# A written-out transfer order: other groups of tiles, in another order

## The chip, the cores and the metric

One core of a Trainium2 chip runs the whole problem. The metric is the time of one launch on the device in microseconds (us), smaller is better. A core has five engines with a queue of instructions each: TensorE (PE in the profile) multiplies and transposes, VectorE (DVE) and ScalarE (ACT) and GpSimd (POOL) work on elements, and SyncE (SP) issues the transfers here. Sixteen DMA engines move the data between the chip's memory (DRAM) and the on-chip buffer. Each transfer of this kernel is spread over all sixteen.

## The reference

```
x:         16 x 512 x 1024  float32      weight: 1024 x 768  float32
add_value: 16 x 512 x 768   float32      scale = 0.1
out = (scale * matmul(x, weight) + add_value)   float32, 16 x 512 x 768
```

The rows of the sixteen batches form one matrix of 8192 rows. So the kernel reads 33.6 MB of x, 25.2 MB of add_value and 3.1 MB of weight, and writes 25.2 MB of out.

## The kernel before, in words

**Tiles.** The 8192 rows are cut into 64 tiles of 128 rows. Partition p holds rows 64p to 64p+63, and tile t is row 64p+t of each partition (lines 57 to 59). Tiles that follow each other therefore lie side by side in DRAM within each partition: one transfer of n tiles of x takes one contiguous run of n times 4 KB for each of the 128 partitions, and n times 3 KB for add_value and out. In the trace each such run is one packet.

**Rings.** x is loaded into `xs`, a ring of 24 slots (X_SLOTS, line 23); tile t uses slot t modulo 24. add_value is loaded into `ao`, another ring of 24 slots (A_SLOTS). VectorE writes the result over the add_value that it read, in the same slot, and the store of out leaves from there. So a slot of `xs` is free again when its tile has been cast, and a slot of `ao` only when the store of the tile 24 before has landed.

**The order of transfers** is written out by hand in `STREAM` (lines 12 to 21): ("x", s, n) loads tiles s to s+n-1 of x, "a" the same of add_value, "w" one of the eight slices of weight (through slots 16 to 23 of `ao`), "o" stores tiles of out, and "l" and "r" store the two column parts of the last tile. The loop at line 231 walks through it. It issues every transfer on SyncE (lines 93, 241, 247 and 255), and ahead of a transfer it emits as many computing steps as must have been emitted before: for an "x" over slots used earlier, until the old tiles have been cast (line 237); for an "o", until its last tile is finished (line 251). SyncE works in order: a transfer that waits for its slots holds up all transfers behind it. The order of instructions on the other engines is nearly independent of `STREAM`; what changes is when their data arrives.

**The steps.** The first three tiles (EARLY) are multiplied weight slice by weight slice as the weights arrive (function `head`), and their scaled product waits in slots 13 to 15 of `ao` until add_value comes (`added`, line 228). Every later tile is a `step` (line 204). Sixteen matmuls (`product`, line 161) multiply the tile with the weight, and in the middle of them the next tile is turned: GpSimd casts it to bf16 (line 129), TensorE transposes it in four pieces (line 139), ScalarE copies it out of PSUM (line 145). For the eighteen tiles in `PAIRS` VectorE turns the tile instead (lines 102 and 113). Then VectorE scales, adds and writes (`finish`, line 169). Products have three PSUM buffers, so TensorE can run up to about two tiles ahead of a `finish` that waits for add_value.

Of the kernel before, what the change touches and what calls it, by code (L numbers as in the profile page):

```python
# [11 lines left out]
STREAM = [  # L12
    ("x", 0, 1), ("x", 1, 1), ("x", 2, 1), ("w", 0, 1), ("w", 1, 1), ("w", 2, 1),
    ("w", 3, 1), ("w", 4, 1), ("w", 5, 1), ("x", 3, 1), ("w", 6, 1), ("w", 7, 1),
    ("a", 0, 3), ("x", 4, 3), ("a", 3, 7), ("x", 7, 3), ("x", 10, 6), ("a", 10, 6),
    ("x", 16, 8), ("a", 16, 8), ("x", 24, 7), ("o", 0, 8), ("o", 8, 8), ("a", 24, 5),
    ("x", 31, 7), ("a", 29, 4), ("x", 38, 5), ("a", 33, 5), ("o", 16, 8), ("x", 43, 5),
    ("a", 38, 7), ("x", 48, 8), ("o", 24, 8), ("a", 45, 3), ("a", 48, 6), ("o", 32, 8),
    ("x", 56, 8), ("a", 54, 6), ("o", 40, 8), ("o", 48, 4), ("a", 60, 4), ("o", 52, 6),
    ("o", 58, 4), ("o", 62, 1), ("l", 63, 1), ("r", 63, 1),  # L20
]

X_SLOTS = 24
# [267 lines left out]
```

## Time and profile before

| what | us |
|---|---|
| median of four runs (213.49, 213.86, 214.08, 215.13) | 213.97 |
| the profiled execution's own time | 213.49 |
| its span, first to last instruction | 211.7 |
| what lies around the span | 1.8 |
| TensorE busy in the span | 195.7 |
| mean rate of the transfers over the span | 412 GB/s |
| bytes moved by SyncE's queue | 87.03 MB |

How it is read: the profile is one execution. Busy times of engines overlap, so they are compared with the span and not added up. The queue row of the profile gives the share of the span in which the sixteen DMA engines had a packet of that queue in work. The windows view gives the same for stretches of the span, with the granted share of TensorE's clock in the third column from the right. The chain of waits follows back from the last instruction what released each step.

### The profile page before, as it was taken

To read this page: it belongs to the slowest core of one execution; us is meant where nothing else is said; L and a number is where in the kernel's file an instruction comes from. 1 tells how busy PE (TensorE), PEld (TensorE's weight loads), DVE (VectorE), ACT (ScalarE), POOL (GpSimd) and SP (SyncE) were. 2 spreads that over 40 slices of the span, in tenths; PEclk is the share of its full clock that TensorE was granted. 3 is DMA by queue.
4 is the path that set the end of the run, shared out by engine and by line. 5 is a ranking of instruction groups with operands and counts; after the bars stand their busy time and mean duration, and the time that the engine had idled before them with its cause. 6 is when DMAs were issued, how large, how long until landed. Compare 5 with 4: busy or idle time off the path is not lost.

```text
span 211.7 us, 3011 instructions
## 1 busy us (share of the span) xinstructions
PE 195.7 (92%) x1195; PEld 119.9 (57%) x1218; DVE 130.8 (62%) x223; ACT 49.3 (23%) x52; POOL 63.4 (30%) x69
## 2 busy tenths in 40 slices
PE   7777499999999999999999999999999997999991
PEld 2544356666565666566566665565656664655650
DVE  1447113359788699679786983699787981053241
ACT  3503112333203113013031121130230310313310
POOL 1310505290260260900804407105408102713000
PEclk9999669999999999999999999999999999999999
DMA  6999999999999999999999999999999999999984
GB/s 243 390 424 426 450 430 404 433 456 418 441 409 424 446 441 410 430 431 418 435 418 442 442 427 432 429 421 437 362 352 410 440 443 404 428 404 428 437 374 190
DMA packets 6637, 87.21 MB, mean 412 GB/s; under 512 B 736, under 2 KB 864, under 8 KB 2656
## 3 DMA queue, kind: packets, MB, share of 16 engines
q1 hardware_dynamic: 6624, 87.03, 97.9%
q8 instruction: 9, 0.15, 0.3%
q14 instruction: 4, 0.03, 0.0%
HBM read 61.87 MB, written 25.17 MB: 411 GB/s over the span
## 4 chain that ended last, share of the span: by engine, by line
DMA 54%; PE 40%; SPq 2%; DVE 1%; issue 1%; POOL 0%; POOLq 0%; DVEq 0%
DMA out_dram<-ao 37%; PE mm L161 35%; DMA ao<-in_add_value_dram 7%; DMA xs<-in_x_dram 6%; PE tp L139 5%; DMA ao<-in_weight_dram 3%; DVE ao L169 1%; SPq L241 1%; POOL xb L129 0%; SPq L93 0%; SPq L247 0%; SPq L255 0%; POOLq L129 0%; DVEq L169 0%
## 5 line engine op out<-in xcount | busy, mean ns | idle before, releaser
L161 PE MATMUL mm<-w_bf,xt 128*128 128x256 bf16 (+1 forms) x719 | 129.2, 329 | 3.7 <-DVE w_bf L97 1.3
L161 PEld LDWEIGHTS <-xt 128*128 128x128 bf16 x736 | 69.5, 99 | 53.2 <-ACT xt L145 10.8
L169 DVE SCALAR_TENSOR_TENSOR ao<-mm,ao 128x768 f32<-128x768 f32 (+2 forms) x62 | 58.3, 944 | 62.0 <-PE mm L161 30.8
L145 ACT COPY xt<-tp 128x1024 bf16<-128x1024 bf16 (+1 forms) x49 | 46.6, 961 | 152.0 <-PE tp L139 151.9
L113 DVE STREAM_TRANSPOSE vt<-vx 32x256 f32<-32x256 f32 x144 | 62.7, 435 | 2.9 <-POOL vx L102 0.7
L129 POOL CAST xb<-xs 128x1024 bf16<-128x1024 f32 x43 | 43.3, 1040 | 44.5 <-DMA xs<-in_x_dram 36.5
L161 PE MATMUL mm<-w_bf,vt 128*128 128x256 bf16 (+1 forms) x282 | 49.1, 325 | 0.3
L102 POOL CAST vx<-xs 128x1024 bf16<-128x1024 f32 x18 | 18.2, 1040 | 81.5 <-DVE vt L113 46.9
L161 PEld LDWEIGHTS <-vt 128*128 128x128 bf16 x288 | 28.2, 98 | 17.5
L139 PE MATMUL tp<-identity,xb 128*128 128x128 f32 x184 | 28.6, 279 | 6.0 <-POOL xb L129 5.1
L139 PEld LDWEIGHTS tp<-identity,xb 128*128 128x128 f32 x184 | 22.2, 145 | 12.6 <-POOL xb L129 5.8
L97 DVE CAST w_bf<-ao 128x768 bf16<-128x768 f32 x8 | 4.5, 562 | 4.7 <-DMA ao<-in_weight_dram 4.7
L87 PE MATMUL warm<-zeros 128*128 128x512 bf16 x10 | 4.4, 628 | 1.2 <-DVE zeros L75 1.2
L125 DVE CAST xb<-xs 128x512 bf16<-128x512 f32 x3 | 1.3, 426 | 5.1 <-DMA xs<-in_x_dram 5.1
L87 PEld LDWEIGHTS <-zeros 128*128 128x128 bf16 x10 | 1.3, 140 | 3.4 <-issue 2.2
L127 POOL CAST xb<-xs 128x512 bf16<-128x512 f32 x2 | 1.7, 866 | 5.0 <-DMA xs<-in_x_dram 5.0
L228 DVE TENSOR_TENSOR ao<-ao 128x768 f32<-128x768 f32 x3 | 2.7, 948 | 0.0
L197 DVE TENSOR_SCALAR ao<-mm 128x768 f32<-128x768 f32 x2 | 1.8, 952 | 1.1 <-PE mm L161 1.1
L127 ACT ACT_TABLE_LOAD x1 | 1.3, 1283 | 0.7 <-PEq L272 0.7
L127 ACT CAST xb<-xs 128x512 bf16<-128x512 f32 x1 | 0.6, 618 | 2.1 <-DMA xs<-in_x_dram 2.1
L194 ACT ACTIVATE ao<-mm 128x768 f32<-128x768 f32 x1 | 0.8, 817 | 0.0
L75 DVE MEMSET zeros<- 128x256 uint32 x1 | 0.3, 272 | 0.9 <-PEq L272 0.9
(6 smaller groups left out, 0.9 us busy)
## 6 DMA issues: line engine op xcount, KB each, us to landing
out_dram<-ao SPq DMA_DIRECT2D x6, 3072.0 KB, 25.6
xs<-in_x_dram SPq DMA_DIRECT2D x3, 4096.0 KB, 26.6
xs<-in_x_dram SPq DMA_DIRECT2D x2, 3584.0 KB, 33.3
ao<-in_add_value_dram SPq DMA_DIRECT2D x3, 2304.0 KB, 15.8
ao<-in_add_value_dram SPq DMA_DIRECT2D x2, 2688.0 KB, 16.0
xs<-in_x_dram SPq DMA_DIRECT2D x2, 2560.0 KB, 30.5
ao<-in_add_value_dram SPq DMA_DIRECT2D x2, 1920.0 KB, 19.1
ao<-in_weight_dram SPq DMA_DIRECT2D x8, 384.0 KB, 7.6
```

The lines of the kernel that those rows point to most:

```text
L87: nc.tensor.matmul(warm[:, 0:CUT], zeros[:, 0:P], zeros, start=True, stop=True)
L97: nc.vector.tensor_copy(w_bf[:, j + i, :], ao[:, s + i, :])
L102: nc.gpsimd.tensor_copy(vx[:, i, :], xs[:, (t0 + i) % X_SLOTS, :])
L113: nc.vector.transpose(vt[b:b + 32, :, 32 * a:32 * a + 32], pairs[32 * a:32 * a + 32, :, b:b + 32])
L127: other(xb[:, K // 2:K], src[:, K // 2:K])
L129: nc.gpsimd.tensor_copy(xb, src)
L139: nc.tensor.transpose(tp[:, c, :], pairs[:, c * P:(c + 1) * P], identity)
L145: nc.scalar.copy(dst[:, c:c + q, :, :], src[:, c:c + q, :, :])
L161: nc.tensor.matmul(mm_tiles[t, cols[0]][:, n0:n1], lhs(t, j), w_bf[:, j, n0:n1], start=(j == 0), stop=(j == KJ - 1))
L169: nc.vector.scalar_tensor_tensor(a, mm_tiles[t, part][:, n0:n1], float(scale), a, op0=mybir.AluOpType.mult, op1=mybir.AluOpType.add)
L228: nc.vector.tensor_add(ao[:, t, :], ao[:, EARLY_AT + t, :], ao[:, t, :])
L241: nc.sync.dma_start(xs[:, k:k + n, :], x_v[:, s:s + n, :])
```

## The change

Only `STREAM` is changed, from its thirteenth entry on; everything else, line numbers included, stays. The head (three tiles of x, weight, a fourth tile of x, the first three tiles of add_value) and the last three stores are the same. Between them the tiles are cut otherwise: loads and stores of x, add_value and out now hold four or eight tiles and begin at a tile number, and so at a ring slot, that is a multiple of four, except for one load of a single add_value tile (tile 3) and a store of two tiles at the end. The order among loads of x, loads of add_value and stores is another one as well. There are 47 transfers in place of 46.

```
-    ("a", 0, 3), ("x", 4, 3), ("a", 3, 7), ("x", 7, 3), ("x", 10, 6), ("a", 10, 6),
-    ("x", 16, 8), ("a", 16, 8), ("x", 24, 7), ("o", 0, 8), ("o", 8, 8), ("a", 24, 5),
-    ("x", 31, 7), ("a", 29, 4), ("x", 38, 5), ("a", 33, 5), ("o", 16, 8), ("x", 43, 5),
-    ("a", 38, 7), ("x", 48, 8), ("o", 24, 8), ("a", 45, 3), ("a", 48, 6), ("o", 32, 8),
-    ("x", 56, 8), ("a", 54, 6), ("o", 40, 8), ("o", 48, 4), ("a", 60, 4), ("o", 52, 6),
-    ("o", 58, 4), ("o", 62, 1), ("l", 63, 1), ("r", 63, 1),
+    ("a", 0, 3), ("x", 4, 4), ("a", 3, 1), ("a", 4, 4), ("x", 8, 4), ("x", 12, 4),
+    ("a", 8, 8), ("x", 16, 8), ("a", 16, 8), ("x", 24, 8), ("o", 0, 8), ("o", 8, 8),
+    ("a", 24, 4), ("x", 32, 4), ("a", 28, 8), ("a", 36, 4), ("x", 36, 8), ("o", 16, 8),
+    ("x", 44, 4), ("a", 40, 8), ("x", 48, 4), ("o", 24, 8), ("x", 52, 8), ("a", 48, 4),
+    ("o", 32, 8), ("a", 52, 4), ("a", 56, 8), ("x", 60, 4), ("o", 40, 8), ("o", 48, 8),
+    ("o", 56, 4), ("o", 60, 2), ("o", 62, 1), ("l", 63, 1), ("r", 63, 1),
```

## The prediction

> **What bounds the kernel now.** I read the page's totals and its queue row, then the rate in stretches, then the waits of SyncE, then TensorE's timeline, then single packets.
>
> ```profile
> span 211.7 us, 3011 instructions
> PE 195.7 (92%) x1195; PEld 119.9 (57%) x1218; DVE 130.8 (62%) x223; ACT 49.3 (23%) x52; POOL 63.4 (30%) x69
> ...
> q1 hardware_dynamic: 6624, 87.03, 97.9%
> ```
>
> Both the DMA engines (97.9%) and TensorE (92%) are nearly full, so I have to find which of them sets the end. The stretches (wall time, busy time of each engine, granted clock, DMA share, GB/s):
>
> ```profile
> 23.10:29.92 6.82, 5.87 (x20) 3.39 (x22) 0.00 (x0) 1.01 (x1) 2.64 (x3) 0.50 1.00 425
> ...
> 60.00:90.00 30.00, 29.79 (x189) 18.54 (x192) 24.57 (x45) 6.07 (x6) 11.79 (x12) 1.00 1.00 425
> 90.00:120.00 30.00, 29.79 (x189) 18.46 (x192) 24.47 (x45) 6.07 (x6) 9.97 (x11) 1.00 1.01 430
> ...
> 150.00:160.00 10.00, 9.95 (x64) 6.05 (x64) 7.84 (x16) 3.04 (x3) 0.74 (x2) 1.00 1.00 350
> 160.00:180.00 20.00, 18.44 (x117) 11.21 (x117) 13.18 (x23) 3.04 (x3) 5.83 (x7) 1.00 1.00 430
> ```
>
> The rate is 425 to 430 GB/s for most of the run and 350 in 150 to 160. That hole is worth (430-350)/430 x 10 = 1.9 us. What stands there:
>
> ```profile
> 122.71 0.38 SPq L255 DMA_DIRECT2D out_dram<-ao  x1
> 123.14 28.42 SPq L247 DMA_DIRECT2D ao<-in_add_value_dram  x2
> 151.66 0.37 SPq L255 DMA_DIRECT2D out_dram<-ao  x1
> ```
>
> SyncE issues a(45,3) at 123.14 and holds a(48,6) until 151.23, because tiles 48 to 53 take the slots of o(24,8), which lands only then. Behind that store just 2.8 us of work is queued, a(45,3). Most DMA engines run dry and start again together at 152.2.
>
> TensorE has only these pauses after 24 us:
>
> ```profile
> 23.83 1.11 PE L139 MATMUL tp<-identity,xb 128*128 128x128 f32 x4 [3.61 <-POOL xb L129]
> ...
> 179.94 0.66 PE L139 MATMUL tp<-identity,xb 128*128 128x128 f32 x4 [1.45 <-POOL xb L129]
> ...
> 185.74 1.46 PE L161 MATMUL mm<-w_bf,xt 128*128 128x512 bf16 x8 [0.78 <-DVE ao L169]
> ```
>
> The first waits for x(4,3); the two late ones (2.23 us) are x(56,8) and a(54,6) arriving late after the hole.
>
> **Prices from packets.** A packet of 4096 B usually takes 159 ns, 12288 B 460, 24576 B 912, 32768 B 1213: 27.2 GB/s an engine plus 8 ns. An odd size at an odd slot costs no more: most packets of a(10,6) (slot 10, 18432 B) take 686 to 694 ns against 686 by the formula. An engine has 8 packets of each transfer and a 9 ns semaphore write. Its share is 5,439,488 B, 200.0 us; 46 x 8 x 8 ns = 2.9 and 46 x 9 ns = 0.4 make 203.3.
>
> The engine that ends last is behind this running sum by 4.3 us at 30 us (1.7 us start, slow first packets, instruction fetches of about 1 us), 4.1 at 150.7, 6.3 at 161.2 (end of a(48,6)), 7.1 at 199.3 and 7.0 at its end, 210.34. Its packets of a(48,6) took 7.7 us where 5.5 are due, and a(54,6) and a(60,4) cost 0.9 more. So the last DMA engine sets the end, and 3.05 us of it is slow reads after 151. TensorE would allow an earlier end: its last store is issued at 207.41, and the engines that lag least are through with it at 208.95, 1.54 later.
>
> **What the skill says.** "DMA: Bandwidth & Descriptors", "Where 436 GB/s comes from", puts the ceiling of sixteen engines at 435 GB/s; 16 x 27.2 = 435 agrees, so larger transfers can gain only the 8 ns a packet. The same page, "Why a DMA increments its semaphore by 16 and not by 1", says that a transfer counts as landed when the last of its engines is done; the trace agrees: o(24,8) landed at 151.22, while the first engine had gone on at 148.63. "TensorE: Matmul & The Clock Gate", Part 1, says that TensorE runs at half clock after an idle window of some 3.4 us and needs a busy window to recover; the trace agrees, with 0.50 from 23.10 to 29.92 around a pause of 3.61 us.
>
> **The change, part by part.**
>
> *Packets.* 47 transfers for 46: one more time 73 ns. The sum becomes 203.41. Larger groups save nothing in number.
>
> *x(4,4) for x(4,3).* 16 KB for 12 KB a packet is +1.22 us until the first of these tiles can be cast, so TensorE restarts at 25.05 and not 23.83. If the half clock still ends at 29.92, it costs (29.92-25.05)/2 = 2.43 instead of 3.05. Net for TensorE: +0.6; +1.2 if the window shifts with the restart.
>
> *The front.* a(8,8) waits for `added` like a(10,6) did (22.2), but 15 us of loads are queued by then. x(8,4) lands by about 34.7 (sum 30.15 + 4.1 + 0.45 from last packet to semaphore), needed for tile 8 at 40. x(24,8) waits for one cast more, tile 7, about 28; the queue reaches to 61.
>
> *The waits in the middle.* For each load held by a store, I compare that store's landing (running sum + 4.55; the first engine is through at sum + 2.0) with the work queued behind it:
> - a(28,8) waits for o(8,8): sum 83.67, landing 88.2. a(24,4) and x(32,4) behind it keep the first engine busy until 94.2.
> - a(40,8) waits for o(16,8): 120.25, landing 124.8. x(44,4) keeps it busy until 127.1; the new packets need 1.0 after issue (151.23 to 152.19), so 125.8. Margin 1.3.
> - a(48,4) waits for o(24,8): 144.64, landing 149.2, and x(52,8) (9.7 us) is queued, to 156.3. This is where the old order ran dry; margin 6.
> - a(56,8) waits for o(32,8): 165.34, landing 169.9, first packets 170.9; a(52,4) ends on the first engine at 171.0. Margin 0.1, the tightest.
>
> So the hole at 151 is gone and a near one stands at 171.
>
> *TensorE's supply.* x(36,8) lands at 117.5; casts of 39 and 40 (2.1 us) go before that of 36 on GpSimd, so its transpose can start at 120.7, due about 121.0: margin 0.3. x(60,4) lands at 185.8 against 193.8. a(48,4) lands at 162.6, 2 us after tile 48's product, which the PSUM buffers cover. SyncE's extra issue (0.4) lies under queued work. The two late pauses go: 206.94-2.23+0.6 = 205.3 for TensorE's last matmul, last store issued 205.8, done 207.3.
>
> *The end.* Last DMA engine: 203.41+4.05+e = 207.46+e, where e is what slow reads are left. That is next late after TensorE's 207.3. The unknown is e: 0 if the common restart made the packets slow, 3.05 if they come anyway. I take 0.4, half of what a(54,6) and a(60,4) showed, because before 150 reads of every size were at full rate. So 207.9; +1.33 from last packet to span's end (211.68-210.34) = 209.2; +1.82 = 211.0 against 213.49 of the profiled execution. The median lies 0.48 above that execution, so I predict 211.4.
>
> **Rivals.**
> - *The stall moves to 171* (24%). A margin of 0.1 is less than the spread of the engines; they run dry there and a(56,8) reads as slowly as a(48,6) did. e = 3 again: 210.5+1.33+1.82+0.48 = 214.1, no change. For it: the same shape of wait. Against: only the first engines idle, and for tenths.
> - *TensorE becomes the bound* (8%). The longer pause keeps the clock at half one window more, 3.41 us, which costs 1.7: last matmul 207.0, store done 209.05, time 212.2+0.48 = 212.7. That still is slightly faster.
> - *Slow reads belong to the late tiles of add_value* (16%). All slow loads after 150 are of tiles 48 and up, while x(56,8) ran at full rate. At a(48,6)'s 2.23/6 = 0.37 us a tile, a(48,4), a(52,4) and a(56,8) would cost 16 x 0.37 = 5.9: 207.46+5.9+3.63 = 217.0, slower. It is slower than the 0.5% bound from 0.25 us a tile on (e = 4). Against it: a(54,6) and a(60,4) cost only 0.09 a tile.
> - *Alignment itself counts.* If slots or multiples of four changed packet times, a(10,6) would show it; it doesn't, so I give it nothing.
>
> **The numbers.** Forecast 52%, alone 210.5 to 212.6 (e from 0 to about 1.2, with or without the median's offset); the rivals as given. Range 210.3 to 214.8, into the first and last rival. A measurement here can tell about 0.5% (1.1 us) from no change. Faster 0.60 (forecast and TensorE's), no change 0.24, slower 0.16.
>
> **What would show it.** Right: no wait of the DMA engines near 150, rates of 425 or more between 150 and 180, no pause of TensorE after 26 us, last matmul near 205.3. Wrong: a rate under 400 after 150, above all in a(56,8); TensorE pausing at 120 for x(36,8); half clock beyond 31.

## The result, and the profile after

The changed kernel takes 213.45 us (median of 40 executions, 211.14 to 216.88) against 214.25 us of the kernel before (61 executions, 212.69 to 216.27). The ratio is 0.9939, 95% interval 0.9922 to 0.9957. Ratios here leave out executions more than 1.5% above their kernel's fastest (11 of these 40, 3 of the 61), while medians and the lowest and highest are of all, so a kernel with many long executions looks better by its ratio than by its median. By the medians alone it is 0.9963: the kernel is faster, by some 0.4 to 0.6%. Forecast was 211.4; of a gain of 2.6 us, 0.8 came. The profiled execution took 212.23 us, span 210.3.

The totals of the page, of the changed kernel:

```profile
span 210.3 us, 3009 instructions
PE 194.9 (93%) x1195; PEld 119.2 (57%) x1218; DVE 131.2 (62%) x223; ACT 49.3 (23%) x52; POOL 63.5 (30%) x69
...
q1 hardware_dynamic: 6768, 87.03, 98.2%
```

Both full resources are a little fuller. The stretches of the changed kernel (columns as before: wall, five engines, granted clock, DMA share, GB/s):

```profile
60.00:90.00 30.00, 29.79 (x189) 18.52 (x192) 24.57 (x46) 6.07 (x6) 11.77 (x13) 1.00 0.99 423
90.00:120.00 30.00, 29.79 (x190) 18.50 (x192) 22.91 (x42) 6.07 (x6) 8.49 (x9) 1.00 1.01 432
...
150.00:160.00 10.00, 9.95 (x66) 6.15 (x66) 7.84 (x15) 3.04 (x3) 0.74 (x1) 1.00 0.98 420
160.00:170.00 10.00, 9.95 (x66) 6.14 (x65) 6.90 (x13) 2.02 (x2) 6.31 (x7) 1.00 1.00 427
170.00:180.00 10.00, 9.95 (x65) 6.26 (x64) 6.67 (x11) 1.73 (x2) 1.72 (x2) 1.00 1.00 392
180.00:190.00 10.00, 9.89 (x65) 6.16 (x65) 3.14 (x4) 3.33 (x4) 2.80 (x4) 1.00 1.02 420
```

The hole of 150 to 160 (350 GB/s before) is filled: 420. A new one stands in 170 to 180, at 392. SyncE's issues there:

```profile
149.78 20.60 SPq L247 DMA_DIRECT2D ao<-in_add_value_dram  x2
170.47 0.76 SPq L241 DMA_DIRECT2D xs<-in_x_dram  x1
171.32 34.11 SPq L255 DMA_DIRECT2D out_dram<-ao  x7
```

a(52,4) goes out at 149.78, a(56,8) only at 170.05, when o(32,8) has landed. Its first packets start at 171.01. Four of the packets of a(56,8) took 2.8 to 3.0 us and two more 2.3 to 2.5, where 0.91 is due.

TensorE has one pause left after 19 us, the one for x(4,4):

```profile
24.82 1.12 PE L139 MATMUL tp<-identity,xb 128*128 128x128 f32 x4 [4.82 <-POOL xb L129]
```

From there to its last matmul it does not stop for longer than 0.25 us. The late pauses of 1.45 and 0.78 us are gone.

### The profile page after: what moved, and what is told of

It reads as the page before. It is cut to its first block, busy times and chain, and to the rows that moved or that the text cites. A ratio compares the mean times of both kernels' runs of the same rounds, so it can differ in the third digit from the quotient of the medians.

```text
span 210.3 us, 3009 instructions
## 1 busy us (share of the span) xinstructions
PE 194.9 (93%) x1195; PEld 119.2 (57%) x1218; DVE 131.2 (62%) x223; ACT 49.3 (23%) x52; POOL 63.5 (30%) x69
## 4 chain that ended last, share of the span: by engine, by line
PE 84%; DMA 10%; SPq 1%; issue 1%; POOL 0%; ACT 0%; DVE 0%; POOLq 0%; ACTq 0%
PE mm L161 75%; PE tp L139 9%; DMA xs<-in_x_dram 7%; DMA ao<-in_weight_dram 3%; SPq L241 1%; POOL xb L129 0%; ACT xt L145 0%; SPq L93 0%; DVE ao L169 0%; POOLq L129 0%; ACTq L145 0%
```

## The experiments

**How a load is judged.** From the packets of a trace I take, for each load, what its packets took beyond 8 ns plus bytes at 27.2 GB/s, summed and divided by the sixteen engines: the *excess* of this load. After the first 10 us nearly all loads have 0.00 to 0.20 us, in every kernel here, and most of them under 0.10. In the kernel before, a(48,6) has 1.78; in the changed one a(56,8) has 0.89 and x(60,4), which follows it, 0.39. A *slow packet* is one that took over 0.1 us too long. The last engine can collect more than the mean.

**Theories.** *Restart*: where so little is queued behind a store that DMA engines run dry before the load that waits for the store starts, the loads from there on read slowly. *Place*: the late tiles of add_value are slow to read. *Noise*: slow reads come by chance. Others are named where they came up.

**1. Fill the tight place at 171.**

```
-    ("a", 52, 4), ("a", 56, 8), ("x", 60, 4),
+    ("a", 52, 4), ("x", 60, 4), ("a", 56, 8),
```

> The changed kernel with one swap: x(60,4) goes ahead of a(56,8), so that 4.9 us more of work is queued when a(56,8) waits for the store o(32,8). Restart theory (engines that run dry and start again together read slowly): the packets of a(56,8) fall from up to 3.0 us back to 0.91 us, the rate in 170 to 180 goes from 392 to about 430 GB/s, and the time goes to about 210.8 to 211.3, some 2 us under the median of the changed kernel. Place theory (late tiles of add_value are slow to read): a(56,8) and x(60,4) stay slow by about 1.6 us, time as the changed kernel, 213.4. Noise theory (slow reads come by chance): the slow packets move elsewhere and the median stays at 213.4.

Measured: 211.43 us (six executions, 211.19 to 213.80), ratio to the kernel before 0.9896 (0.9857 to 0.9936). The stretches of this kernel:

```profile
170.00:180.00 10.00, 10.00 (x65) 6.12 (x64) 7.14 (x12) 1.12 (x2) 1.22 (x2) 1.00 1.03 440
182.00:186.00 4.00, 4.00 (x28) 2.54 (x27) 0.63 (x1) 1.01 (x1) 1.04 (x1) 1.00 1.04 436
```

440 where the changed kernel has 392; a(56,8) has an excess of 0.12 instead of 0.89, and x(60,4) 0.01 instead of 0.39. The median lies 0.1 us above the expected 210.8 to 211.3, and one execution of the six was at 213.80. One swap of two loads, with the same bytes, the same transfers and the same tiles, gives the rest of the forecast gain. The place theory, by which these tiles would stay slow, falls.

**2. Fill the hole of the kernel before, and nothing else.**

```
-    ("a", 38, 7), ("x", 48, 8), ("o", 24, 8), ("a", 45, 3), ("a", 48, 6),
+    ("a", 38, 7), ("x", 48, 4), ("o", 24, 8), ("x", 52, 4), ("a", 45, 3), ("a", 48, 6),
```

> The kernel before with one entry split: x(48,8) becomes x(48,4) ahead of o(24,8) and x(52,4) behind it, so that 7.7 us of work and not 2.8 us is queued when a(48,6) waits for that store. Restart theory: no hole of rate in 150 to 160 (425 or more, before 350), a(48,6) at 686 ns a packet, time 211.3 to 212, about 2 us under the kernel before (214.2). Place theory: a(48,6) stays slow by about 2 us and the time stays within 0.5 us of the kernel before. Noise theory: the same time as before, slow packets somewhere else.

Measured: 211.81 us (211.24 to 212.29), ratio 0.9901 (0.9871 to 0.9931). The stretch of this kernel that was at 350:

```profile
150.00:160.00 10.00, 10.00 (x64) 5.90 (x62) 7.44 (x15) 3.04 (x3) 0.47 (x1) 1.00 1.03 439
```

The old order with its odd sizes, unaligned slots and x(4,3) gains about as much as any version of the new one. Multiples of four are worth nothing by themselves that these intervals could tell; what counts is what is queued behind each store that a load waits for.

**3. The same hole, other rows.**

```
-            nc.sync.dma_start(ao[:, k:k + n, :], add_v[:, s:s + n, :])
+            f = s - 48 if s >= 48 else s
+            nc.sync.dma_start(ao[:, k:k + n, :], add_v[:, f:f + n, :])
```

> The kernel before with the three late loads of add_value (tiles 48 to 63) taken from the rows of tiles 0 to 15 instead: the output of those tiles uses other rows of add_value, the order, sizes, slots and waits are the same. Restart theory: the load after the hole at 151 still has some 50 packets over 0.1 us too long and the rate in 150 to 160 is again about 350 GB/s. Place theory: packets at 686 ns, rate above 400 in that stretch except for the dry time.

Measured: 214.09 us in one execution. The stretch of this kernel:

```profile
150.00:160.00 10.00, 10.00 (x67) 6.15 (x66) 7.83 (x16) 3.04 (x3) 0.77 (x1) 1.00 0.98 343
```

The load after the hole has an excess of 1.69 us with 53 slow packets (1.78 and 56 before), though it reads the rows of tiles 0 to 5. (The last sixteen tiles of out then are not those of the reference.) So it isn't the rows.

**4. A hole where there was none.**

```
-    ("x", 44, 4), ("a", 40, 8), ("x", 48, 4), ("o", 24, 8),
+    ("x", 44, 2), ("a", 40, 8), ("x", 46, 2), ("x", 48, 4), ("o", 24, 8),
```

> The changed kernel with a hole put in where there was none: x(44,2), a(40,8), x(46,2), x(48,4) in place of x(44,4), a(40,8), x(48,4). Behind o(16,8) only 2.4 us is queued while a(40,8) waits for it to land, so most engines run dry near 124 for about a us. Restart theory: a(40,8), whose packets took 0.91 us, reads slowly (many packets over 1 us, rate of 125 to 135 under 390), and about 2 us are lost there beyond the dry time. Noise theory: tiles 40 to 47 read at full rate, only the dry time of at most 1 us on the early engines shows.

x(46,2) and x(48,4) are two transfers because one of six tiles would run over the end of the ring (slots 22 to 27 of 24).

Measured: 216.30 us in one execution. The stretches of this kernel:

```profile
124.00:136.00 12.00, 12.00 (x79) 7.39 (x77) 11.05 (x21) 2.02 (x2) 4.99 (x5) 1.00 0.93 375
136.00:148.00 12.00, 11.83 (x78) 7.21 (x76) 8.98 (x16) 3.04 (x3) 1.81 (x2) 1.00 1.03 401
```

In the changed kernel:

```profile
124.00:136.00 12.00, 11.89 (x76) 7.39 (x77) 10.99 (x21) 2.02 (x2) 4.98 (x5) 1.00 1.00 427
136.00:148.00 12.00, 11.76 (x74) 7.07 (x74) 9.04 (x17) 3.04 (x3) 4.75 (x5) 1.00 1.04 443
```

a(40,8) has an excess of 0.58 us, and x(48,4) behind it 1.10, in the middle of the run and on other tiles. The short load between them, x(46,2), has 0.00. Slow reads can be called up by a hole, at a place of my choice: the noise theory falls as the main cause. The expectation missed one thing: more is lost in a load *behind* the one that restarted. And 216.30 holds a second loss: the tight place at 171 stayed in this kernel, and the two loads there have 0.54 and 1.14.

**5. A deeper hole at 171.**

```
-    ("a", 52, 4), ("a", 56, 8), ("x", 60, 4),
+    ("a", 52, 3), ("a", 55, 9), ("x", 60, 4),
```

> The changed kernel with the cut between two loads moved by one tile: a(52,3), a(55,9) in place of a(52,4), a(56,8). Work queued behind o(32,8) shrinks from 3.7 to 2.8 us, so the DMA engines run dry near 171 by 0.9 us more, on more engines, in every run. Restart theory: slow reads in every run, time 213.8 to 214.5 with little spread, above the 213.4 median of the changed kernel. If the dry time alone counted and not the restart: about 0.5 us over the faster runs of the changed kernel, 212.6. Noise theory: same as the changed kernel, spread over 211 to 215.

Measured: 213.36 us (22 executions, 212.11 to 215.34), ratio 0.9965 (0.9943 to 0.9987). That misses the restart theory's number: with 0.9 us less queued the median is that of the changed kernel (213.45, and 213.87 in experiment 10) and not more, and the spread stays wide. The intervals of the ratios overlap, so a growth of the loss with the dry time isn't shown; the margin of 0.1 us of the changed kernel is already on the bad side. Its trace, of one of the longer executions (214.52), shows where the loss sits now. The second line is this kernel, the third the changed one:

```profile
170.00:180.00 10.00, 10.00 (x65) 6.27 (x64) 7.35 (x13) 1.01 (x1) 1.04 (x1) 1.00 1.02 422
182.00:186.00 4.00, 4.00 (x29) 2.65 (x27) 1.92 (x2) 1.01 (x1) 0.00 (x0) 1.00 1.04 311
...
182.00:186.00 4.00, 4.00 (x28) 2.49 (x27) 0.96 (x1) 1.59 (x2) 0.00 (x0) 1.00 1.05 408
```

Not in a(55,9) (excess 0.32), but in x(60,4) behind it: 1.32 us, 41 slow packets.

**6. Fill 171 with a quarter of it.**

```
-    ("a", 52, 4), ("a", 56, 8), ("x", 60, 4),
+    ("a", 52, 4), ("x", 60, 1), ("a", 56, 8), ("x", 61, 3),
```

> The changed kernel with one tile of x, x(60,1), put ahead of a(56,8) and x(61,3) behind it: 1.3 us more queued at 171. Restart theory: that is enough, since the margin was 0.1 us, and the time is that of the kernel with all of x(60,4) ahead, 211.4 (211.0 to 211.8), with a(56,8) at 0.91 us a packet. If the order of x(60,4) mattered by itself (an earlier arrival of x), only a quarter of the gain or none would come: 212.9 to 213.4.

Measured: 212.22 us, three of six executions at 211.17 to 211.49, the others at 212.95, 215.07 and 215.39. The median missed the expected 211.0 to 211.8. In its trace (an execution of 211.17) a(56,8) and x(61,3) have an excess of 0.03 and 0.02. So a quarter of the load can be enough, but this run doesn't show that it is so each time.

**7. Fill 171 with a store.**

```
-    ("a", 56, 8), ("x", 60, 4), ("o", 40, 8),
+    ("o", 40, 4), ("a", 56, 8), ("x", 60, 4), ("o", 44, 4),
```

> The changed kernel with the margin at 171 filled by a store and not by x: o(40,4) ahead of a(56,8), o(44,4) behind x(60,4). 3.7 us more is queued at 171, while x(60,4) still is the last load, with stores behind it. Restart theory: both a(56,8) and x(60,4) run at full rate (0.91 and 0.61 us a packet) and the time is 211.3 to 211.8. Theory of the last load (16 KB packets of x(60,4) are slow in themselves, or ahead of stores): a(56,8) is at full rate, x(60,4) still loses 1 to 1.5 us, time 212.2 to 213.

Measured: 211.63 us (211.02 to 212.54), ratio 0.9878 (0.9839 to 0.9917); excess 0.01 in a(56,8) and 0.08 in x(60,4). x(60,4) comes as late as before, with stores behind it, and reads at full rate. The last load isn't slow by itself.

**8. Cut x(60,4) at its place.**

```
-    ("a", 56, 8), ("x", 60, 4), ("o", 40, 8),
+    ("a", 56, 8), ("x", 60, 1), ("x", 61, 3), ("o", 40, 8),
```

> The changed kernel with x(60,4) cut in two at the same place: x(60,1), x(61,3) in place of x(60,4), nothing queued earlier. Restart theory: no change, median 213.0 to 213.8, slow packets at 171 and after it. Theory that the 16 KB packets of four tiles of x are slow: the excess of 1 to 1.5 us in x(60,4) goes, 212.0 to 212.4.

Measured: 214.03 us over all six executions, which lie from 210.94 to 215.45. That spread is too wide to place it. The trace is of its slowest execution, so for the place at 171 I take from it only what the cut was to show: x(61,3), now in packets of 12 KB, still has an excess of 1.23 us. The size of the packets doesn't make it.

**9. Give TensorE its early start back, with 171 filled.**

```
-    ("x", 4, 4), ("a", 3, 1), ("a", 4, 4), ("x", 8, 4),
+    ("x", 4, 3), ("a", 3, 1), ("a", 4, 4), ("x", 7, 5),
```

> The changed kernel with x(60,4) ahead of a(56,8) and, besides, x(4,3), x(7,5) in place of x(4,4), x(8,4), which lets TensorE restart 1.2 us earlier. If the last DMA engine sets the end then: 211.4, as with the swap alone. If TensorE does: 0.6 to 1.2 us less, 210.2 to 210.8.

Measured: 211.95 us (211.18 to 213.92), ratio 0.9896 (0.9844 to 0.9948). TensorE's pause shrinks from 4.82 to 3.62 us in its trace, and the time is no better than with the swap alone. The lever was weaker than meant, though: TensorE's last matmul ends at 205.42, only 0.3 us before that in the trace of experiment 1 (205.76), after small pauses elsewhere. The last packets say more: here the last engine ends its part of o(60,2) at 207.10, and the three stores behind it at 208.05, 208.69 and 209.04, with nothing between but the time of their packets. It is busy to the end, while TensorE is done 3.6 us before. This trace shows something else, in 136 to 148:

```profile
124.00:136.00 12.00, 11.89 (x77) 7.60 (x78) 11.05 (x21) 2.02 (x2) 4.98 (x5) 1.00 1.01 425
136.00:148.00 12.00, 11.78 (x75) 7.07 (x75) 9.05 (x17) 3.04 (x3) 4.06 (x5) 1.00 1.02 412
...
182.00:186.00 4.00, 4.00 (x29) 2.68 (x28) 0.28 (x1) 1.01 (x1) 1.04 (x1) 1.00 1.04 449
```

a(40,8), which had a margin of 1.3 us at 124, has an excess of 0.24, and x(48,4) behind it 0.78. In the other traces with this margin x(48,4) has at most 0.20, but for the slowest execution of experiment 8 (0.99). This is a second tight place, which bites now and then. When it does can be read from the traces. a(40,8) is issued once the last engine is through with o(16,8), so it is issued later when that engine lags more: in the trace of experiment 8 this engine ends o(16,8) at 125.86 and a(40,8) goes out at 126.35, in the first trace of the changed kernel at 124.14 and 124.61. The first engine ends x(44,4) at nearly the same time in both, 127.29 and 127.03. The margin of 1.3 us had shrunk to 0.9 us here, and to nothing in that execution of experiment 8.

**10. The changed kernel again,** unchanged, for more traces.

> The changed kernel once more, unchanged, for a second execution in the trace: its times fall in two groups, about 212.1 and about 214.3. Restart theory: when this execution is of the second group, the slow packets of a(56,8) and behind it are more or longer than in the first trace (the last engine more than 1.6 us late from there on), and nothing before 170 differs. Clock theory: TensorE's half clock near 25 us lasts longer, its last matmul ends near 206.5 or later.

> The changed kernel unchanged, one more execution for the trace. Restart theory: its time follows the sum of the slow packets from 171 on, about 210.6 plus what the last DMA engine loses there (1.6 us at 212.2; some 3.5 us at 214.3); nothing before 170 differs from the other executions by more than 0.5 us.

> The changed kernel unchanged beside its two variants, on the same chip: median 213.0 to 213.8, between 211 and 215. If the median lies below 212.4 here, the gains of the filled variants are to be read against that and not against 213.4.

Measured: 212.39 and 211.72 us in single executions, and 213.87 us (22 executions, 211.24 to 215.68), ratio 0.9948 (0.9925 to 0.9970). The trace of the third is of an execution of 213.28 us:

```profile
170.00:180.00 10.00, 9.95 (x63) 5.94 (x62) 7.12 (x12) 1.50 (x2) 1.60 (x2) 1.00 1.01 422
182.00:186.00 4.00, 3.95 (x27) 2.48 (x26) 1.83 (x2) 1.01 (x1) 0.00 (x0) 1.00 1.04 346
```

In all four traces of this kernel the two loads after the tight place lose over 1 us together: 0.89 + 0.39, 0.19 + 1.19, 0.24 + 0.88, 0.23 + 0.94, with the larger part mostly in x(60,4). From a(52,4) to the end the last engine loses 1.46, 1.31, 1.40 and 1.98 us. That doesn't order the four times (212.23, 212.39, 211.72 and 213.28), because the engine was 4.20, 4.63, 3.89 and 4.78 behind the sum already at the end of a(52,4): executions differ before 170 too, by more than the expected 0.5 us. The half clock of the first (25.2 to 28.6) is shorter than in the profile shown above (22.6 to 29.4) and its time is no better, which speaks against the clock theory as well. I caught no trace near 214.3 of the unchanged kernel.

**11. Fill 124, and fill both.** Only ("x", 48, 1) goes ahead of a(40,8), with x(49,3) behind it; in the second kernel the swap of experiment 1 as well.

```
-    ("x", 44, 4), ("a", 40, 8), ("x", 48, 4), ("o", 24, 8),
+    ("x", 44, 4), ("x", 48, 1), ("a", 40, 8), ("x", 49, 3), ("o", 24, 8),
```

> The changed kernel with x(48,1) ahead of a(40,8) and x(49,3) behind it, so that 1.3 us more is queued when a(40,8) waits for o(16,8) (margin 2.6 us and not 1.3); the tight place at 171 is left. Two places theory (the tight queue at 124 starts slow reads in some executions, that at 171 in most): the times above 214 get rare, the fastest stay, median 212 to 212.6. One place theory (171 alone): no change, 213.0 to 213.8.

> The changed kernel with both tight places filled: x(48,1) ahead of a(40,8), and x(60,4) ahead of a(56,8). Two places theory: all executions between 210.8 and 212, median 211.2, and no stretch of the trace under 405 GB/s between 120 and 200. One place theory: as with the swap at 171 alone, 211.4 with single times of 213 to 215 in between. If slow reads come by chance as well, single slow executions stay here too.

> The swap at 171 alone once more, beside the version with both places filled: median 211.3 to 211.9. Two places theory: one execution in five or six above 213, from slow reads that begin between 124 and 140. One place theory: none.

Measured beside each other and beside the third of experiment 10:

| kernel | us | lowest to highest | ratio to before |
|---|---|---|---|
| changed | 213.87 | 211.24 to 215.68 (22) | 0.9948 (0.9925 to 0.9970) |
| 124 filled | 212.95 | 212.57 to 216.16 (6) | 0.9932 (0.9911 to 0.9952) |
| 171 filled | 211.77 | 211.00 to 212.40 (6) | 0.9878 (0.9853 to 0.9903) |
| both filled | 211.54 | 210.89 to 212.32 (6) | 0.9875 (0.9849 to 0.9900) |

Filling 171 is worth 2.1 us. Filling 124 lowers the excess of the load behind it to 0.03 and 0.05 in the two traces, but its median missed the expected 212 to 212.6, one execution was at 216.16, and with 171 filled it adds nothing that these intervals can tell. Nor did the two-places theory's slow executions come with 171 alone filled: none of these six lies above 213. With both filled two of six lie above the expected 212, at 212.22 and 212.32. The trace with 124 alone filled still has the loss at the end, and that with both has not:

```profile
170.00:180.00 10.00, 9.95 (x65) 6.27 (x65) 6.88 (x11) 1.01 (x1) 1.04 (x1) 1.00 1.00 420
182.00:186.00 4.00, 4.00 (x29) 2.71 (x28) 1.20 (x2) 1.01 (x1) 0.00 (x0) 1.00 1.04 324
```

```profile
170.00:180.00 10.00, 9.95 (x64) 6.28 (x64) 7.42 (x13) 1.01 (x1) 1.04 (x1) 1.00 1.03 437
182.00:186.00 4.00, 4.00 (x29) 2.67 (x28) 0.30 (x1) 1.01 (x1) 1.04 (x1) 1.00 1.04 442
```

The two kernels with 171 filled beat the kernel before and the changed one. With 124 alone filled the kernel beats the one before, but its interval overlaps that of the changed one.

Single executions say the same: above 213 us are 41 of the 64 of the changed kernel and 4 of the 36 of the kernels with 171 filled (experiments 1, 6, 7, 9, 11).

**What stands together.** The *margin* is the work queued beyond the moment at which the waiting load can start. It is given as reckoned by the running sum of the prediction, and as the traces have it: the end of the transfer ahead on the first engine, less the issue of the load, less the 0.96 us that passed between issue and first packet at 171 (170.05 to 171.01). The excess is that of the waiting load and of the load behind it together; for the hole put in, of x(48,4) in place of the short x(46,2).

| place, kernel | margin reckoned, us | margin in the traces, us | excess of the two loads, us |
|---|---|---|---|
| 171, filled (experiments 1, 6, 7, 9, 11) | 1.4 to 5 | 1.5 to 4.8 | 0.02 to 0.13 |
| 151, filled (experiment 2) | 4.1 | 4.0 | 0.07 |
| 124, filled | 2.6 | 2.1 and 2.8 | 0.12 and 0.10 |
| 124, as changed (nine traces) | 1.3 | 1.1 to 1.5 | 0.08 to 0.33 |
| 124, experiment 9 | 1.3 | 0.9 | 1.02 |
| 124, experiment 8 | 1.3 | 0.0 | 1.76 |
| 171, as changed (four traces) | 0.1 | -0.2 to 0.0 | 1.1 to 1.4 |
| 151, kernel before | -0.8 | -0.8 | 1.8 |
| 171, deeper hole | -0.8 | -0.6 | 1.6 |
| 124, hole put in | -1.1 | -1.6 | 1.7 |

By the margin in the traces the rows fall into two groups, with a steep step near 1 us: at 1.1 and more the loads lose at most 0.33 us, at 0.9 and less 1.0 to 1.8. So engines need not run dry for it. In the trace of experiment 10 at 211.72 us no engine had to wait for its first packet at 171, and in experiment 9 none by more than 0.05 us at 124; the loads read slowly all the same. What these have in common with the holes is that little was queued when the load was issued.

## Why the prediction was wrong in size

**What held.** The sum of an engine's packets (203.41) and the lag of the last engine: when a(52,4) ended in the profiled execution it was 4.2 us behind the sum, 4.05 was taken. The hole at 151 went, with margin to spare. TensorE restarted at 24.82 (forecast 25.05), its half clock ended at 29.42, both late pauses went, and x(36,8), with its margin of 0.3, held nothing up. TensorE's last matmul ended at 204.61 (forecast 205.3), and the last store was issued at 205.10 (forecast 205.8; this execution's head ran about 0.2 earlier). "The last DMA engine sets the end" held too: the last engine ended its part of o(60,2) at 207.13 and worked through the three stores behind it without a pause, to 209.07.

**The step that failed** is "The unknown is e ... I take 0.4". The last engine came to its end at 209.07, 5.66 us behind the sum, so e is 1.6 in the profiled execution. A second term was too small as well: the median lies 1.22 us above that execution, where 0.48 was taken. In the trace of experiment 10 with 213.28 us, nearer to the median, the last store lands 1.1 us later, and half of that is lost after a(52,4).

The working had found the place: "a(56,8) waits for o(32,8) ... Margin 0.1, the tightest". But it went on as if a margin above zero were enough, set the stall at 171 at 24%, and argued against it that "only the first engines idle, and for tenths". The place was reckoned well: first packets at 171.01, forecast 170.9. In the four traces the margin was -0.2 to 0.0; in one no engine waited, in the others two to four did, by up to 0.7 us. The runs show that this was enough for the two loads to lose 1.1 to 1.4 us, and that they lose at most 0.13 at the same place with a margin of 1.5 us or more.

**The likeliest case and its rival, then.** The time lies between the forecast (211.4) and "the stall moves to 171" (214.1), nearer to the rival, and the place is the rival's. Its form was other: the rival had engines run dry and a(56,8) read as slowly as a(48,6); in three of four traces most of the loss is in x(60,4) behind it. With 171 filled, and nothing else changed, the medians come to 211.4 to 211.8, close to the forecast. That is in part luck: in the trace of experiment 1 the last engine ends 5.08 us behind the sum, so e is 1.0 and not 0.4, and the median lies 0.1 us below that execution and not 0.48 above it.

**The other rivals.** "Slow reads belong to the late tiles of add_value" is refuted by experiments 1 and 3. "TensorE becomes the bound" is refuted by the traces: the half clock lasted no longer than before (6.8 us), and TensorE's last matmul ended at 204.61, not at 207.0. "Alignment itself counts" is refuted as far as the time goes by experiment 2: 211.81 with the odd sizes.

**What stays open.** Why reads are slow when a load is issued to a nearly empty queue isn't settled, and the step near 1 us rests on few traces. The traces show longer packets, 6 to 56 of the 128 of a load, for some 2 to 8 us, partly only in a load behind, after some 8 us of packets at full rate; stores at these places have an excess of at most 0.05 us. What holds these packets up is not in the traces. Nor is it settled what makes single executions of filled kernels take 213 to 216 us (experiments 1, 6, 11), nor how much the place at 124 costs on the median.

## What to carry to other kernels

Where one queue feeds all DMA engines and the last of them sets the end, walk the order through with a running sum, and note for each transfer that waits for another how much is queued beyond the moment at which it can start. Put some microseconds there: with 2 us and more, as the traces have it, loads lost at most 0.13 us here, with 1.1 to 1.5 at most 0.33, and 0.1 as reckoned cost as much as a dry queue. A reckoned margin also has to cover the lag of the last engine, which ate 1.3 us of it in one execution. Such a repair is one swap of two loads: worth 2.0 us here, where the whole new order gave 0.8.

## What was not expected of the hardware

A queue that is nearly empty costs not the gap but what follows. Gaps of nothing to some 2 us, on none to twelve of the sixteen engines, were followed by loads whose packets took up to 3.0 us where 0.91 is due, and in most traces by more loss still in a load behind, up to 16 us after the gap, at a share of the DMA engines that still shows as full (1.04 at 311 GB/s). A full DMA share is therefore no proof of full rate: the GB/s column has to be read beside it.
